# RWKV state update: GpSimd decays the old state and VectorE adds the chunk's products, in place of TensorE's copies of the state into PSUM

## The chip, the cores and the metric

One core of one Trainium2 chip runs the whole program. The time is device microseconds (us) of one execution. Engines are named as in the profile: PE is TensorE (PEld its weight loads), DVE is VectorE, ACT is ScalarE, POOL is GpSimd, SP is SyncE, which here issues DMAs.

## The reference, cut to what matters

The program is a stack of blocks (feed-forward layers, one RWKV mixer, one convolution mixer, two attention and retention blocks). The change lies in the RWKV mixer alone. It has 12 heads of 64 and scans a 64x64 state over 256 context tokens and then 256 latent tokens, once forwards and once backwards:

```python
def wkv_scan(S0, r, w, k, v, kk, bb, reverse):
    ...
    def step(S, inp):
        rt, wt, kt, vt, kkt, bt = inp
        sk = jnp.einsum('bhij,bhj->bhi', S, kkt)
        S = S * wt[:, :, None, :] - sk[..., None] * bt[:, :, None, :] + vt[..., None] * kt[:, :, None, :]
        return S, jnp.einsum('bhij,bhj->bhi', S, rt)

    S, ys = lax.scan(step, S0, xs, reverse=reverse)
    return S, jnp.moveaxis(ys, 0, 1)
...
    for d in range(2):
        ...
        S_c, yc = wkv_scan(S0, r_c, w_c, kd_c, v_c, kk_c, b_c, reverse=(d == 1))
        _, yl = wkv_scan(S_c, r_l, w_l, kd_l, v_l, kk_l, b_l, reverse=(d == 1))
```

## The kernel before, in words

The scan is done in chunks of 64 tokens (`CH`), in float32. Two heads stand together on the 128 partitions (index `x`, 64 partitions each), so there are six pairs of heads, `f` from 0 to 5. For each pair three functions run. `wkv_prepare` makes the pair's projections (the g matmuls on the normed input `y0`, two float16 halves), decays, keys and queries. `wkv_inverse` makes the chunks' 64x64 triangular inverses `SC`: products of keys (KRbd, KBT), 32x32 transposes and a serial loop of small additions on DVE (tiles N and tm), and then small 32x32 matmuls in bank n with ACT copies between them. `wkv_apply` carries the state through eight chunks, `n` from 0 to 7: four of context and four of latents. Both directions `d` go along in each chunk.

One chunk of `wkv_apply`, a step from here on, is a serial chain. PE multiplies the old state (`Sbd` in the trace) by the chunk's keys (tile KR) into bank `b`; ACT copies that into R; PE multiplies R by SC; ACT copies the result into VU; PE multiplies VU by KB into a second bank, `sb`; DVE reads `sb`, multiplies by the chunk's decay `PC`, and writes the new state, from which the next step starts. In the kernel before the old state is in `sb` already: four matmuls by the identity matrix (`ident`) put it there, and the KB products are added to it in PSUM. The state is block diagonal for the two heads, and kept for six chunks (`at` names the buffer of each).

The order on each engine is not written out. A list scheduler places the instructions of all three functions by its own estimates, and each engine then runs its list in order. So while `wkv_apply` of one pair waits in its chain, the projections of the next pair or the out projection, and the key products and transposes of the next inverse, fill PE; they are called fillers below. In the trace all these matmuls have line 232 or 235 (the helpers `mm` and `tr`).

Of the kernel before, what the change touches and what calls it, by code (L numbers as in the profile page):

```python
# [12 lines left out]
OP = mybir.AluOpType  # L13
# [3 lines left out]
P = 128  # L17
# [8 lines left out]
CH = 64  # L26
# [189 lines left out]
class Program:  # L216
# [371 lines left out]
    def run(self):  # L588
        nc, tc, ins = self.nc, self.tc, self.ins
        with ExitStack() as es:  # L590
            self.const = es.enter_context(tc.tile_pool(name="const", bufs=1))
            self.small = es.enter_context(tc.tile_pool(name="small", bufs=1))
            self.psum = es.enter_context(tc.tile_pool(name="ps", bufs=1, space=PSUM))
            self.banks, self.turn, self.bufs = self.BANKS, {}, {"x": 1, "y": 1}
            self.M = [self.const.tile([P, 72, 2], F32, name=f"M{l}") for l in range(2)]
            self.Hl = self.const.tile([P, KD, S], F32, name="Hl")
            self.ones = self.const.tile([P, P], F32, name="ones")
            self.ident = self.const.tile([P, P], F32, name="ident")
            self.eps6 = self.const.tile([P, 1], F32, name="eps6")
            nc.vector.memset(self.ones, 1.0 / D)  # L600
            nc.vector.memset(self.eps6, 1e-6)
            nc.sync.dma_start(self.ident, ins["k_a"][:, 0:P])
            self.sel = self.const.tile([P, 2], F32, name="sel")
            nc.scalar.dma_start(self.sel, ins["k_s"])
            self.craw = self.const.tile([P, KD, 32], F32, name="craw")
            self.cpad = self.const.tile([P, KD, 32], F16, name="cpad")
            self.rst = self.const.tile([P, S], F32, name="rst")
            with ExitStack() as es2:
                E = self.E = {"zi": 0}
                ypool = es2.enter_context(tc.tile_pool(name="y0", bufs=1))  # L610
                opool = es2.enter_context(tc.tile_pool(name="o", bufs=1))
                t = lambda shape, name, dt=F32, pool=ypool: pool.tile(list(shape), dt, name=name)
                self.y0 = t([P, KD, 512], "y0h", F16), t([P, KD, 512], "y0l", F16)
                E["la"], E["reset"] = t([P, 512], "la"), t([P, S], "reset")
                E["zpad"] = [t([P, 2, S + 2], f"zpad{i}") for i in range(2)]
                E["hm"], E["om"] = t([P, 20], "hm"), t([P, 20], "om")
                t([P, 198], "gap")
                E["o"] = t([P, KD, S], "oh", F16, opool), t([P, KD, S], "ol", F16, opool)
                E["sg"] = t([P, S], "sg", F32, opool)
                nc.gpsimd.memset(E["reset"], 1.0)  # L620
                nc.gpsimd.memset(E["reset"][:, ::CH], 0.0)
                for z in E["zpad"]:
                    nc.gpsimd.memset(z, 0.0)
                self.first()
                self.even()
            self.rest()
            self.output()
# [489 lines left out]
    def wkv_apply(self, f):  # L1117

        nc, E = self.nc, self.E
        (SC, SR), (KB, VU), St = E.pop(("chunks", f)), E.pop(("tokens", f)), E["S"]  # L1120
        KR, PC, bon = E["KR", f], E["PC", f], E["bon", f]
        lo = slice(64, 128)
        at = (0, 1, 0, 2, 3, 4, 5)
        uix = lambda q, d, x, c: ((q * 2 + d) * 2 + x) * 4 + c
        for n in range(8):
            q, c = (1, n) if n < 4 else (0, n - 4)
            b = self.bank("w")
            for d in range(2):
                for x in range(2):
                    self.mm(b[lo, d * P + x * CH : d * P + x * CH + CH], SC[0:64, uix(q, d, x, c), 0:64],  # L1130
                            VU[0:64, d, q, c, x * CH : x * CH + CH], d == 0 and x == 0, n == 0)
            for d in range(2):
                if n:
                    self.mm(b[lo, d * P : d * P + P], KR[:, d, q * S + c * CH : q * S + c * CH + CH], St[:, at[n - 1], d, :], False, True)
            if n < 7:
                sb = self.bank("w")
                for x in range(2):
                    h = slice(64 * x, 64 * x + 64)
                    for d in range(2):
                        if n:  # L1140
                            self.mm(sb[h, d * CH : d * CH + CH], self.ident[:, h], St[:, at[n - 1], d, h], d == 0, False)
            R = self.tmp([P, 256], "R")
            nc.scalar.copy(R[lo], b[lo, 0:256])
            for d in range(2):
                for x in range(2):
                    o = d * P + x * CH
                    self.mm(b[lo, 256 + o : 256 + o + CH], SC[lo, uix(q, d, x, c), :], R[lo, o : o + CH], d == 0 and x == 0, True)
            nc.scalar.copy(VU[lo, :, q, c, :], b[lo, 256:512].rearrange("p (d m) -> p d m", d=2))
            if n == 7:
                break  # L1150
            for x in range(2):
                h = slice(64 * x, 64 * x + 64)
                for d in range(2):
                    self.mm(sb[h, d * CH : d * CH + CH], KB[:, d, q, c, h], VU[:, d, q, c, h], n == 0 and d == 0, True)
            for x in range(2):
                h = slice(64 * x, 64 * x + 64)
                nc.vector.tensor_tensor(St[h, at[n], :, h], sb[h, : 2 * CH].rearrange("p (d i) -> p d i", d=2),
                                        PC[h, n, :].unsqueeze(2).to_broadcast([64, 2, CH]), op=OP.mult)
        yb = self.bank("w")
        for cn in range(4):  # L1160
            tt, hh = cn // 2, cn % 2
            rows = slice(64 * hh, 64 * hh + 64)
            o = tt * P
            for d in range(2):
                c = cn if d == 0 else 3 - cn
                self.mm(yb[rows, o : o + P], KR[:, d, 512 + c * CH : 512 + c * CH + CH], St[:, at[3 + c], d, :], d == 0, False)
                for x in range(2):
                    self.mm(yb[rows, o + x * CH : o + x * CH + CH], SR[:, uix(0, d, x, c), :],
                            VU[:, d, 0, c, x * CH : x * CH + CH], False, d == 1)
        y4 = yb[:, :S].rearrange("p (h i) -> p h i", h=4)  # L1170
        mu = self.tmp([P, 4], "mu")
        nc.vector.tensor_reduce(mu, y4, axis=AX.X, op=OP.add)
        nc.vector.tensor_scalar(mu, mu, 1.0 / 64, None, op0=OP.mult)
        yc = self.tmp([P, 4, 64], "yc", bufs=1)
        nc.vector.tensor_tensor(yc, y4, mu.unsqueeze(2).to_broadcast([P, 4, 64]), op=OP.subtract)
        sq = self.tmp([P, 4, 64], "of", bufs=1)
        nc.scalar.activation(sq, yc, AF.Square)
        var = self.tmp([P, 4], "var")
        nc.vector.tensor_reduce(var, sq, axis=AX.X, op=OP.add)
        nc.vector.tensor_scalar(var, var, 1.0 / 64, 64e-5, op0=OP.mult, op1=OP.add)  # L1180
        nc.gpsimd.tensor_tensor(var, var, E["half"].to_broadcast([P, 4]), op=OP.pow)
        nc.vector.tensor_tensor(yc, yc, var.unsqueeze(2).to_broadcast([P, 4, 64]), op=OP.mult)
        tb = self.bank("w")
        for t in range(2):
            self.tr(tb[:, t * P : t * P + P], yc[:, 2 * t : 2 * t + 2, :].rearrange("p h i -> p (h i)"))
        self.mm(tb[:, S:], E["gup", f], E["sg"], False, True)
        of = self.tmp([P, S], "of", bufs=1)
        nc.vector.scalar_tensor_tensor(of, tb[:, :S], self.v("e_gn_w", f, 1), bon, op0=OP.mult, op1=OP.add)
        nc.vector.tensor_tensor(of, of, tb[:, S:], op=OP.mult)
        self.split(E["o"][0][:, f, :], E["o"][1][:, f, :], of)  # L1190
# [716 lines left out]
```

## Time and profile before

| | |
|---|---|
| median of 3 runs | 2735.37 us (2731.1 to 2735.75) |
| the profiled execution's own time | 2735.91 us |
| its span in the profile | 2734.1 us |
| granted TensorE clock, mean | 0.968 |
| PE busy | 2619.9 us, 96% |
| DVE busy | 1749.9 us, 64% |
| ACT busy | 1278.9 us, 47% |
| POOL busy | 423.5 us, 15% |
| the six pairs' steps and inverses | from about 525 to 960 us of the span |

Busy time is the time in which an engine had an instruction in hand. The granted clock is the share of full speed that TensorE was given (1.0 is 2.4 GHz, 0.5 is 1.2 GHz). Matmuls of float32 have two records each in the trace.

### The profile page before, as it was taken

Reading aid. Unit: us, or ns where it says so; the run is one execution under the profiler, and the core shown is the slowest. Engines: PE = TensorE matmul, PEld = TensorE weight load, DVE = VectorE, ACT = ScalarE, POOL = GpSimd, SP = SyncE. Lnnn points to the kernel's source line nnn. Section 1 sums busy time; section 2 is a strip of 40 time slices with the busy share of each in tenths; the row PEclk is TensorE's granted clock in tenths of the full one; section 3 lists DMA queues with packets and bytes.
Section 4 is the critical chain, followed back from the end, with each engine's and each line's share of the span. In section 5 each row is a group of like instructions: output and inputs, shape, how many; then the busy total and the mean of one; then the engine's idle time right before and its main releaser. Section 6 shows DMA issues by size and latency. Waiting matters only on the chain.

```text
span 2734.1 us, 53369 instructions
## 1 busy us (share of the span) xinstructions
PE 2619.9 (96%) x23012; PEld 2009.6 (74%) x23012; DVE 1749.9 (64%) x2601; ACT 1278.9 (47%) x1821; POOL 423.5 (15%) x413
## 2 busy tenths in 40 slices
PE   8999998799999899999989999999999999999998
PEld 4444444476667678888878887888888888888887
DVE  6676676765567366665676556666565666766664
ACT  5454555443344254444645445554544455544443
POOL 0000010321121000199520010000120300000301
PEclk9999999988798899999999999999999999999999
DMA  9676784100102156655626666555656655556563
GB/s 313 240 254 229 263 291 134 53 27 21 32 14 74 40 171 193 208 184 192 182 79 201 193 194 194 169 177 165 214 170 193 200 163 166 171 157 222 170 193 101
DMA packets 427775, 451.71 MB, mean 165 GB/s; under 512 B 9890, under 2 KB 414920, under 8 KB 420243
## 3 DMA queue, kind: packets, MB, share of 16 engines
q1 hardware_dynamic: 422272, 441.29, 50.7%
q10 hardware_dynamic: 5267, 7.01, 0.8%
q8 instruction: 180, 2.95, 0.5%
q14 instruction: 56, 0.46, 0.1%
HBM read 447.18 MB, written 1.08 MB: 164 GB/s over the span
## 4 chain that ended last, share of the span: by engine, by line
PE 60%; DVE 8%; issue 4%; ACT 4%; DMA 2%; POOL 2%; ACTq 0%; SPq 0%; POOLq 0%; DVEq 0%
PE g L232 48%; PE w L232 4%; PE m L232 4%; DVE w L138 3%; PE n L232 2%; ACT w L137 2%; PE m L235 1%; DVE acc L1385 1%; DMA stage<-in_w_in 1%; DVE SC L1057 1%; POOL acc L1391 0%; DMA stage<-in_o_w_in 0%; PE o L232 0%; DVE yl L347 0%; DVE xn L484 0%
## 5 line engine op out<-in xcount | busy, mean ns | idle before, releaser
L232 PEld LDWEIGHTS <-w 128*128 128x128 f16 x14784 | 1440.5, 98 | 447.2 <-issue 96.9
L138 DVE SCALAR_TENSOR_TENSOR w<-stage,w 128x1024 f16<-128x1024 f32 (+2 forms) x812 | 971.6, 1230 | 455.5 <-ACT w L137 453.2
L137 ACT ACTIVATE w<-stage 128x1024 f16<-128x1024 f32 (+2 forms) x812 | 797.7, 1031 | 542.2 <-PE g L232 317.4
L232 PE MATMUL g<-yh,w 128*128 128x256 f16 x5568 | 931.1, 273 | 8.4 <-ACT yh L346 8.3
L232 PE MATMUL g<-yl,w 128*128 128x256 f16 x2784 | 759.1, 273 | 5.6 <-DVE yl L347 5.1
L232 PE MATMUL g<-hh,w 128*128 128x256 f16 (+1 forms) x1936 | 343.0, 282 | 0.0
L232 PE MATMUL g<-hl,w 128*128 128x256 f16 (+1 forms) x968 | 273.4, 282 | 0.0
L232 PE MATMUL g<-y0h,w 128*128 128x512 f16 (+1 forms) x704 | 219.2, 380 | 8.8 <-ACT y0h L346 8.5
L1299 POOL TENSOR_SCALAR diag<-ident,cws 128x128 f16<-128x128 f16 x156 | 144.2, 943 | 8.9 <-DVE cws L1294 8.9
L232 PE MATMUL g<-w,yh 128*128 128x256 f16 (+1 forms) x928 | 138.1, 262 | 0.2 <-ACT ak L1633 0.2
L232 PE MATMUL g<-y0l,w 128*128 128x512 f16 (+1 forms) x352 | 133.8, 381 | 1.3 <-DVE y0l L347 1.3
L232 PE MATMUL g<-w,yl 128*128 128x256 f16 (+1 forms) x464 | 116.5, 262 | 0.0
L311 POOL TENSOR_TENSOR acc<-sq,sq 128x256 f32<-128x256 f32 (+1 forms) x9 | 11.7, 1295 | 625.4 <-ACT sq L753 338.5
L232 PE MATMUL n<-y0h,w 128*128 128x512 f16 x352 | 108.2, 379 | 0.0
L514 ACT ACTIVATE silu<-g 128x512 f32<-128x512 f32 x50 | 29.9, 597 | 155.9 <-issue 135.0
L232 PEld LDWEIGHTS <-yh 128*128 128x128 f16 x928 | 86.9, 98 | 9.4 <-issue 0.9
L232 PE MATMUL g<-ybh,w 128*128 128x256 f16 x512 | 85.2, 273 | 0.0
L516 DVE SCALAR_TENSOR_TENSOR hid<-g,silu 128x512 f32<-128x512 f32 x55 | 38.0, 691 | 68.9 <-PE g L232 64.5
L311 POOL TENSOR_TENSOR acc<-acc,sq 128x256 f32<-128x256 f32 (+1 forms) x45 | 53.9, 1197 | 156.5 <-ACT sq L753 87.4
L1758 POOL TENSOR_TENSOR rst<-rst,epsgn 128x1 f32<-128x1 f32 x16 | 3.0, 189 | 481.4 <-DVE rst L1757 481.4
L232 PE MATMUL g<-ybl,w 128*128 128x256 f16 x256 | 69.8, 273 | 0.0
L311 POOL TENSOR_TENSOR acc<-Hl 128x256 f32<-128x256 f32 x4 | 2.9, 728 | 427.6 <-DVE Hl L1466 427.6
(408 smaller groups left out, 3108.6 us busy)
## 6 DMA issues: line engine op xcount, KB each, us to landing
stage<-in_ffn_w_gu SPq DMA_DIRECT2D x87, 1024.0 KB
stage<-in_ada_w SPq DMA_DIRECT2D x64, 1024.0 KB
stage<-in_w_in SPq DMA_DIRECT2D x64, 1024.0 KB
stage<-in_ffn_w_down SPq DMA_DIRECT2D x32, 1024.0 KB
stage<-in_w_in SPq DMA_DIRECT2D x54, 512.0 KB
stage<-in_w_ffn_gate SPq DMA_DIRECT2D x22, 1024.0 KB
stage<-in_w_ffn_up SPq DMA_DIRECT2D x22, 1024.0 KB
stage<-in_w_ret_proj SPq DMA_DIRECT2D x16, 1024.0 KB
```

The costliest lines, as they stand in the source:

```text
L137: self.nc.scalar.activation(u.t16[:, 0, c], u.stage[:, c], AF.Copy, scale=SW)
L138: self.nc.vector.scalar_tensor_tensor(u.t16[:, 1, c], u.stage[:, c], SW, u.t16[:, 0, c], op0=OP.mult, op1=OP.subtract)
L232: self.nc.tensor.matmul(out, lhsT, rhs, start=start, stop=stop, skip_group_check=True)
L235: self.nc.tensor.matmul(out, in_, self.ident[:k, :k], start=True, stop=True, is_transpose=True, skip_group_check=True)
L311: self.nc.gpsimd.tensor_tensor(acc, state["x"], x, op=OP.add)
L514: nc.scalar.activation(sg, bg, AF.Silu, scale=ISW)
L516: nc.vector.scalar_tensor_tensor(h, bu, ISW, sg, op0=OP.mult, op1=OP.mult)
L1057: nc.vector.transpose(square(h, g), N[quarter(h, g), :, 16 - 16 * g : 48 - 16 * g])
L1299: nc.gpsimd.tensor_scalar(diag[f][:, i, k], id16, w[:, i, k : k + 1], None, op0=OP.mult)
L1385: nc.vector.scalar_tensor_tensor(acc[f], up[:, f, k : k + S], cw[:, f, k : k + 1], acc[f], op0=OP.mult, op1=OP.add)
L1758: nc.gpsimd.tensor_tensor(st[:, 7:8], st[:, 7:8], self.epsgn, op=OP.add)
```

## The change

In chunks 1 to 6 of each pair the four matmuls by the identity go. Two GpSimd instructions per chunk (one for each head) multiply the old state by the chunk's decay into a new tile `kept`, which takes the place of an unused tile of the same size. `sb` then holds the chunk's products alone, and DVE makes the new state as products times decay plus `kept`, in four instructions of 64 columns (head by head, direction by direction), where two of 128 columns stood. Chunk 0 keeps its two DVE instructions.

```diff
@@ run
-                t([P, 198], "gap")
+                E["kept"] = t([P, 198], "kept")[:, :P].rearrange("p (d m) -> p d m", d=2)
@@ wkv_apply
             if n < 7:
                 sb = self.bank("w")
-                for x in range(2):
-                    h = slice(64 * x, 64 * x + 64)
-                    for d in range(2):
-                        if n:
-                            self.mm(sb[h, d * CH : d * CH + CH], self.ident[:, h], St[:, at[n - 1], d, h], d == 0, False)
+                if n:
+
+                    for x in range(2):
+                        h = slice(64 * x, 64 * x + 64)
+                        nc.gpsimd.tensor_tensor(kept[h], St[h, at[n - 1], :, h], PC[h, n, :].unsqueeze(2).to_broadcast([64, 2, CH]), op=OP.mult)
...
-                    self.mm(sb[h, d * CH : d * CH + CH], KB[:, d, q, c, h], VU[:, d, q, c, h], n == 0 and d == 0, True)
+                    self.mm(sb[h, d * CH : d * CH + CH], KB[:, d, q, c, h], VU[:, d, q, c, h], d == 0, True)
...
-                nc.vector.tensor_tensor(St[h, at[n], :, h], sb[h, : 2 * CH].rearrange("p (d i) -> p d i", d=2),
-                                        PC[h, n, :].unsqueeze(2).to_broadcast([64, 2, CH]), op=OP.mult)
+                if n == 0:
+                    nc.vector.tensor_tensor(St[h, at[n], :, h], sb[h, : 2 * CH].rearrange("p (d i) -> p d i", d=2),
+                                            PC[h, n, :].unsqueeze(2).to_broadcast([64, 2, CH]), op=OP.mult)
+                    continue
+                for d in range(2):
+                    nc.vector.scalar_tensor_tensor(St[h, at[n], d, h], sb[h, d * CH : d * CH + CH], PC[h, n, d : d + 1], kept[h, d],
+                                                   op0=OP.mult, op1=OP.add)
```

The scheduler places the program anew. Three places show what it does. The first is PE in the first pair's third chunk, before: `Sbd,KR` are the state's products, `Sbd,ident` the copies, `KRbd,KBT` and `g` fillers, `R,SC`, `VU,KB` and `VU,SC` the rest of the chain.

```order
L232 MATMUL w_4495<-VU_4166,SC_4127 64x64 x4
L232 MATMUL m_4866<-KRbd,KBT_4795 128x256 x2
L232 MATMUL m_4871<-KRbd,KBT_4795 128x256
L232 MATMUL w_4495<-Sbd,KR_4078 64x128 x2
L232 MATMUL w_4502<-Sbd,ident 64x64 x4
L232 MATMUL m_4871<-KRbd,KBT_4795 128x256
L232 LDWEIGHTS w_8_5445
L232 MATMUL g_5470<-y0h,w_8_5445 128x512
L232 MATMUL w_4495<-R_4507,SC_4127 64x64 x4
```

The same place of the changed kernel:

```order
L232 MATMUL w_4495<-Sbd,KR_4078 64x128
L232 MATMUL m_4871<-KRbd,KBT_4795 128x256
L232 MATMUL w_4495<-Sbd,KR_4078 64x128
L232 LDWEIGHTS w_8_5445
L232 MATMUL g_5470<-y0h,w_8_5445 128x512
L232 LDWEIGHTS w_8_5445
L232 MATMUL g_5470<-y0l,w_8_5445 128x512
L232 LDWEIGHTS w_8_5445
L232 MATMUL g_5470<-y0h,w_8_5445 128x512
L232 MATMUL w_4495<-R_4505,SC_4127 64x64 x4
```

The copies are gone, a filler now stands between the two state products, and three g products stand ahead of the R product where one stood.

The second place is PE in the stretch between the fourth pair's steps and the fifth's, where the fifth pair's inverse ends (`T,SC` and `SC,T` are its small matmuls), before:

```order
L232 LDWEIGHTS w_19_7758
L232 MATMUL g_8412<-ol,w_19_7758 128x256
L232 MATMUL n_7377<-T,SC_7125 32x32 x16
L232 MATMUL n_7395<-T,SC_7125 32x32 x16
L232 LDWEIGHTS w_19_7758
L232 MATMUL g_8412<-oh,w_19_7758 128x256
L232 MATMUL n_7413<-SC_7125,T 32x32 x16
L232 MATMUL n_7431<-SC_7125,T 32x32 x16
L232 MATMUL m_7832<-ks_7829,cstA 128x256
L232 MATMUL m_7845<-KRbd,KBT_7791 128x128 x4
```

And in the changed kernel:

```order
L232 MATMUL n_7309<-SC_7125,T 16x16 x64
L232 MATMUL m_7851<-KRbd,KBT_7791 128x128 x4
L232 MATMUL m_7857<-KRbd,KBT_7791 128x256 x2
L232 LDWEIGHTS w_18_7755
L232 MATMUL g_8412<-ol,w_18_7755 128x256
L232 LDWEIGHTS w_18_7755
L232 MATMUL g_8412<-oh,w_18_7755 128x256
L232 MATMUL n_7377<-T,SC_7125 32x32 x16
L232 MATMUL n_7395<-T,SC_7125 32x32 x16
L232 MATMUL m_7862<-KRbd,KBT_7791 128x256
L232 MATMUL n_7413<-SC_7125,T 32x32 x16
L232 MATMUL m_7862<-KRbd,KBT_7791 128x256
```

The long run of g products ahead of `n_7377` (26 in a row before, of which the last stands here) is down to two, and the sixth pair's key products have come in from the fifth pair's steps.

The third place is POOL in the second pair's steps, in the changed kernel (`k`, `v`, `rn` and `kd` belong to the third pair's preparation):

```order
L872 TENSOR_TENSOR k_6209<-zpad_88 128x512
L1142 TENSOR_TENSOR kept<-Sbd,PC_4796 64x128 x10
L872 TENSOR_TENSOR v_6268<-zpad_89 128x512
L944 TENSOR_TENSOR rn_6279<-rn_6279,half 128x8
L1142 TENSOR_TENSOR kept<-Sbd,PC_4796 64x128 x2
L970 TENSOR_TENSOR kd_6304<-kd_6304,k_6209 128x512
```

Before, the same rows stand there without the two of `kept`, in the order k, rn, kd, with v after kd. So the state's 12 GpSimd instructions stand nearly alone in this pair; `rn`, `v` and `kd` wait behind them.

## Rows read from the trace of the kernel before

**Rows 1.** The page: span, and busy time of each engine.

```profile
span 2734.1 us, 53369 instructions
PE 2619.9 (96%) x23012; PEld 2009.6 (74%) x23012; DVE 1749.9 (64%) x2601; ACT 1278.9 (47%) x1821; POOL 423.5 (15%) x413
```

**Rows 2.** Windows: three stretches of steps, then three between; busy us, clock, DMA.

```profile
core 0: us, PE busy (x) PEld busy (x) DVE busy (x) ACT busy (x) POOL busy (x), PEclk, DMA share, GB/s
568.00:608.00 40.00, 39.98 (x382) 26.86 (x383) 27.48 (x72) 15.35 (x31) 4.38 (x4) 1.00 0.06 18
...
788.00:823.00 35.00, 34.94 (x354) 25.63 (x352) 20.80 (x56) 15.70 (x30) 4.35 (x4) 1.00 0.03 9
...
926.50:953.00 26.50, 22.17 (x294) 17.98 (x292) 7.49 (x15) 5.36 (x15) 2.62 (x1) 1.00 0.01 1
```

**Rows 3.** Windows: stretches between the steps of two pairs, same columns.

```profile
608.00:637.00 29.00, 29.00 (x458) 19.53 (x451) 17.38 (x30) 9.89 (x17) 9.09 (x7) 0.57 0.09 24
...
673.00:715.00 42.00, 37.41 (x532) 26.33 (x533) 28.16 (x60) 14.42 (x24) 11.79 (x9) 0.71 0.11 32
...
823.00:863.00 40.00, 36.26 (x550) 26.21 (x548) 30.46 (x64) 17.54 (x29) 11.75 (x9) 0.79 0.34 109
```

**Rows 4.** Timeline: one step of the last pair, with no fillers (start us, us).

```profile
937.94 0.32 PE L232 MATMUL w<-Sbd,KR 128*64 128x128 f32 x1
...
938.69 0.37 ACT L1143 COPY R<-w 64x256 f32<-64x256 f32 x1 [1.96 <-PE w L232]
939.11 0.54 PEld L232 LDWEIGHTS w<-R,SC 64*64 64x64 f32 x8 [0.42 <-ACT R L1143]
...
939.82 0.37 ACT L1148 COPY VU<-w 64x256 f32<-64x256 f32 x1 [0.76 <-PE w L232]
940.24 0.32 PEld L232 LDWEIGHTS w<-VU,KB 128*64 128x64 f32 x8 [0.59 <-ACT VU L1148]
...
940.75 0.59 DVE L1157 TENSOR_TENSOR Sbd<-w,PC 64x128 f32<-64x128 f32 x2 [2.87 <-PE w L232]
941.40 0.13 PEld L232 LDWEIGHTS w<-Sbd,KR 128*64 128x64 f32 x1 [0.23 <-DVE Sbd L1157]
```

**Rows 5.** Timeline: the last pair's last chunk, which has no copies of the state.

```profile
948.31 0.30 PEld L232 LDWEIGHTS w<-Sbd,KR 128*64 128x64 f32 x5 [0.23 <-DVE Sbd L1157]
...
949.05 0.37 ACT L1143 COPY R<-w 64x256 f32<-64x256 f32 x1 [1.96 <-PE w L232]
```

**Rows 6.** Timeline of PE and PEld: a step filled with g products, fourth pair.

```profile
786.86 0.59 PE L232 MATMUL g<-y0h,w 128*128 128x512 f16 x2
787.29 0.38 PE L232 MATMUL g<-y0l,w 128*128 128x512 f16 x1
787.60 0.32 PE L232 MATMUL w<-Sbd,KR 128*64 128x128 f32 x1
...
787.98 0.36 PEld L232 LDWEIGHTS w<-Sbd,ident 128*64 128x64 f32 x4
788.41 0.33 PEld L232 LDWEIGHTS <-w 128*128 128x128 f16 x3
```

**Rows 7.** Timeline of PEld: the same copies at the half clock, third pair.

```profile
722.25 0.66 PEld L232 LDWEIGHTS w<-Sbd,ident 128*64 128x64 f32 x4
```

**Rows 8.** Groups of DVE, 545 to 960 us: busy us, mean ns, idle before.

```profile
L1157 DVE TENSOR_TENSOR Sbd<-w,PC 64x128 f32<-64x128 f32 x84 | 24.2, 288 | 54.1 <-PE w L232 53.2
L138 DVE SCALAR_TENSOR_TENSOR w<-stage,w 128x1024 f16<-128x1024 f32 x17 | 23.5, 1388 | 11.9 <-ACT w L137 11.7
...
L1188 DVE SCALAR_TENSOR_TENSOR of<-w,vec,bon 128x256 f32<-128x256 f32 x6 | 2.9, 483 | 4.8 <-PE w L232 4.7
...
L1175 DVE TENSOR_TENSOR yc<-w,mu 128x256 f32<-128x256 f32 x6 | 2.5, 421 | 0.1
```

**Rows 9.** Groups of POOL, 545 to 960 us, same columns.

```profile
L974 POOL TENSOR_TENSOR KBT<-kd,ep 128x512 f32<-128x512 f32 x9 | 14.5, 1611 | 6.8 <-ACT ep L963 6.5
...
L997 POOL TENSOR_TENSOR ks<-kd,kd 128x256 f32<-128x256 f32 x5 | 3.9, 789 | 0.3
```

More of the change, by code (lines that the diff above doesn't have):

```diff
@@ L1121, in wkv_apply @@
         KR, PC, bon = E["KR", f], E["PC", f], E["bon", f]
+        kept = E["kept"]
         lo = slice(64, 128)
```

## The prediction

> **What bounds the kernel now.** I read the page's head first: the span is 2734.1 us and PE is busy for 96% of it [rows 1]. The change lies in the six pairs' steps, so I read the windows there. In the steps of a pair PE is busy all the time, 39.98 of 40 us and 34.94 of 35, at the full granted clock, while DVE has 20 to 27 us of work and POOL 4 [rows 2]. Only in the last pair's steps, where no fillers are left, PE idles 4.3 of 26.5 us. In the stretches between the steps of two pairs the clock falls to 0.57, 0.71 and 0.79 on average, and PE idles 0, 4.6 and 3.7 us [rows 3]. So the steps are bound by PE's list, not by the chain, except in the last pair; between them it is PE at a lowered clock together with the chain of the inverse (DVE has 30.46 us in 40).
>
> The bare chain stands in the last pair: 3.45 us from one state product to the next (937.94 to 941.40, an idle PE in between) [rows 4]. Of it the DVE update takes 0.59 us, state product to R copy 0.75 us, and R copy to DVE's start 2.06 us.
>
> **What the copies of the state cost.** Chunk 7 has none, and there product to R copy takes 0.74 us [rows 5], with them 0.75 [rows 4]: in the chain they are free. On PE they are not. In a filled step four of the eight loads run after the state products, 0.36 us, and the next filler's load starts behind them (788.41) [rows 6]. At the half clock they take 0.66 us [rows 7]. There are 36 blocks (six chunks, six pairs). In the changed order about seven steps stay without fillers (five of the last pair, two of the fourth), where the freed time is idle time. The other 29 give 29 x 0.36 = 10.4 us, and four that ran at half clock 0.3 us more each: **-11.6 us**.
>
> **The split of the state products.** In 24 steps of the new order a filler stands between the two state products. An entry costs PE: from the last g product to the state product 0.31 us, where a g product takes 0.43 / 2 = 0.215; so 0.095 us, and 0.07 us on the way out (loads end 788.34, next load 788.41) [rows 6]. That is 24 x 0.165 = **+4.0 us**. It is hidden only where PE would wait anyway, and in the steps it hardly does [rows 2]. The Trainium skill, TensorEngine Tiling (Array Packing), Key Properties, says that a change of the tiling mode drains TensorE; state products (128*64) and fillers (128*128) are two modes, so it speaks against this order. The trace agrees, with those 0.095 and 0.07 us; were the drains nothing, the sum would be 4 us better.
>
> **DVE's four instructions for two.** No row has this form. A product of 64 columns from PSUM: 128 columns take 288 ns, 256 take 421 [rows 8], so 1.04 ns a column, and 64 take 221. The nearest row with the same operands (PSUM, a scalar for each partition, an SBUF tile) is L1188, 483 ns for 256 columns, so 283 for 64. Four take 0.88 to 1.13 us, against 0.59. The first state product needs the third of them and the second the fourth, so about 0.22 us of PE's work comes before the end: the bare chain grows by 0.07 to 0.32 us; I take 0.2, as the row with the same operands is the nearer one. In seven bare steps: **+1.4 us** (0.5 to 2.2). In filled steps a filler covers it: the update ends at latest 0.51 + 1.13 = 1.64 us after the start of the KB products, and PE comes to the state product only behind VU,SC and 0.9 to 2.8 us of fillers in the changed order. If that cover were gone, 36 x 0.2 = 7 us. Behind the waiting instruction on DVE stand the next inverse's serial loop and the splits of weights, which PE's fillers wait for; DVE idles 53.2 us in front of this line now [rows 8], and 36 x 0.4 us comes out of that.
>
> **GpSimd.** `kept` needs the old state, ready when the state products start, and DVE needs it 2.81 us later (937.94 to 940.75) [rows 4]. POOL takes 789 ns for 256 columns and 1611 for 512 [rows 9], so 3.2 ns a column and 0.38 us for 128; the upper bound is the 0.79 of 256. A pair takes 0.8 to 1.6 us: 1.2 us or more are to spare. POOL has 4.38 us of work in 40 us of steps [rows 2], and where `kept` stands behind a 1.6 us KBT it is still in time at the lower price. What is queued behind it (rn, v, kd of the next pair) waits for the state at most until the steps end. I cost it at **0**.
>
> **What moved.** Counted in the two orders in products of 512 columns (two of 256 as one), the steps of the six pairs hold 22, 20, 18, 17, 17 and 10 projection products before, and 36, 33, 46, 15, 49 and 3.5 now; the five stretches between hold 27, 46, 35, 50 and 33 before, and 43, 11, 36, 3 and 19.5 now. So 78.5 products go from the stretches into the steps. There they run at the full clock, 78.5 x 0.215 = **+16.9 us**. What the stretches lose is open: at their mean clock of 0.69 a product costs 0.31 us, which would be -24 us; but in two of them 11 and 3 are left, and then DVE's 28 and 30 us [rows 3] bound them. I let the two cancel and take 0.22: **-17.3 us**, bounds 0 and -34 (half clock throughout).
>
> **Sum:** -11.6 + 4.0 + 1.4 + 16.9 - 17.3 = -6.6 us. The profiled execution took 2735.9 us, 0.5 above the median of the runs, so 2729.3; I say **2729**. A measurement of this kernel tells about 0.2%, 5.5 us, from no change.
>
> **The rivals.**
>
> *The moved products pay more than once.* If the stretches shrink by the mean-clock price or the half-clock price, the sum is -13 to -23, 2713 to 2722. For it: all three stretches run at a lowered clock, and one with PE never idle [rows 3]. Against it: DVE's work in the other two.
>
> *The stretches do not shrink (slower).* If the inverse's chain on DVE and ACT already sets their length, the 16.9 us in the steps are simply added: between -6.6 + 17.3 = +10.7 and half of that, 2741 to 2747. It decides from where the stretches give back less than 10.7 us. For it: 30.46 us of DVE in 40, and key products of the next inverse that now stand in the stretch; against it: PE idle there is only 9 to 11% [rows 3].
>
> *GpSimd and DVE hold each other up.* DVE's wide splits (1388 ns [rows 8]) read two SBUF tiles as `kept` does. A pair of `kept` that waits for one of them ends 0.8 + 1.4 = 2.2 to 3.0 us after the state, at the edge of 2.81; and each `kept` can hold a DVE instruction for 0.4 to 0.8 us. In half of the steps, 18 x 0.5 = +9 us: 2738. Against it: 1611 ns for 512 columns is about twice the 789 of 256, so no such surplus shows on average [rows 9]. The Trainium skill, SBUF — State Buffer, SBUF: two separate sides, has VectorE instructions with two SBUF inputs and GpSimd instructions that read SBUF shut each other out for a whole instruction; no row here shows that apart.
>
> *Nothing comes of it.* The freed time turns into waits of PE for the inverse: 2735.
>
> **How the numbers follow.** Forecast 0.42 (its own range 2723 to 2735), moved products pay more 0.22, stretches do not shrink 0.17, hold-up 0.10, nothing 0.09. Faster by over 0.2% (under 2729.9): 0.22 and just over half of the forecast's, 0.45. Slower by over 0.2%: 0.17 and half of the hold-up, 0.22. The rest, 0.33, is within. The range takes in both outer cases but their ends: 2714 to 2744.
>
> **What would show it.** The groups must have no `Sbd,ident`, four DVE instructions of 64 columns a chunk at 0.22 to 0.29 us, and 72 of `kept` at 0.38 to 0.79. The last pair's bare step should be 3.5 to 3.8 us, its DVE update released by PE and not by POOL. In the windows, the steps of the first three pairs and of the fifth should grow by some 1 to 6 us each, and the second and fourth stretch between pairs should shrink. I am wrong if these stretches keep their length, if many updates are released by POOL, or if PE's clock falls within the steps.

## The result and the profile after

The changed kernel took 2750.1 us (median; 2744.9 to 2753.4), the kernel before 2733.3 beside it: ratio 1.0065, 95% interval 1.0048 to 1.0083. It is slower, where 2729 was forecast. The page of after, against [rows 1]:

```profile
span 2742.8 us, 53048 instructions
...
PE 2616.2 (95%) x22724; PEld 2000.4 (73%) x22724; DVE 1760.9 (64%) x2673; ACT 1279.2 (47%) x1821; POOL 450.8 (16%) x485
```

PE has 3.7 us less work and 288 instructions fewer, and the span is 8.7 us longer. So I looked at where PE waits, and at which clock it works. The windows of after follow the work: from a pair's second R copy to its eighth (six steps, odd rows), and on to the next pair's second R copy (the stretch between, even rows). Columns are those of [rows 2].

```profile
568.65:604.62 35.97, 35.17 (x281) 21.39 (x282) 25.14 (x75) 15.58 (x31) 10.41 (x16) 1.00 0.07 19
604.62:642.89 38.27, 33.64 (x539) 22.86 (x537) 24.52 (x48) 15.12 (x24) 8.30 (x9) 0.82 0.12 31
642.89:678.95 36.06, 35.28 (x300) 22.95 (x301) 24.26 (x72) 15.45 (x29) 9.88 (x14) 1.00 0.12 34
678.95:717.56 38.61, 29.76 (x523) 24.21 (x522) 27.33 (x58) 12.92 (x22) 7.42 (x9) 0.73 0.11 31
717.56:752.92 35.36, 34.49 (x281) 20.59 (x281) 26.96 (x75) 17.48 (x32) 13.06 (x18) 1.00 0.06 16
752.92:790.97 38.05, 34.73 (x546) 24.33 (x545) 24.75 (x48) 12.64 (x22) 5.52 (x7) 0.87 0.09 25
790.97:824.16 33.19, 30.36 (x257) 20.26 (x258) 24.20 (x71) 14.79 (x30) 9.78 (x14) 0.93 0.03 9
824.16:865.54 41.38, 35.35 (x521) 28.68 (x520) 25.48 (x51) 10.56 (x19) 6.57 (x7) 0.62 0.01 2
865.54:896.33 30.79, 30.70 (x293) 21.37 (x293) 19.99 (x62) 13.24 (x25) 5.57 (x10) 0.97 0.25 76
896.33:929.08 32.75, 30.70 (x533) 23.09 (x532) 12.98 (x21) 8.56 (x16) 2.97 (x2) 0.69 0.13 44
929.08:956.49 27.41, 21.80 (x182) 17.11 (x182) 6.20 (x25) 4.41 (x13) 6.33 (x13) 0.62 0.00 1
```

The same windows of a kernel that has the old order and the time of before (a_gpsimd_alone, below). I measure against it, since the trace of before itself had more half clock than the other traces of that order (116 us from the first pair's second R copy to the last pair's, against 89 here).

```profile
571.69:603.26 31.57, 31.55 (x287) 20.36 (x284) 23.48 (x63) 13.90 (x28) 6.18 (x13) 1.00 0.06 18
603.26:637.96 34.70, 34.70 (x533) 24.10 (x532) 19.79 (x36) 11.08 (x19) 11.16 (x10) 0.70 0.10 27
637.96:668.21 30.25, 30.23 (x298) 22.10 (x296) 18.36 (x48) 11.71 (x23) 5.33 (x12) 1.00 0.04 15
668.21:712.54 44.33, 38.99 (x586) 28.02 (x584) 29.94 (x69) 17.69 (x29) 13.57 (x12) 0.81 0.10 30
712.54:742.03 29.49, 29.46 (x294) 21.51 (x291) 18.98 (x49) 13.70 (x26) 6.30 (x12) 1.00 0.13 38
742.03:779.95 37.92, 34.39 (x549) 23.46 (x547) 28.20 (x54) 14.85 (x26) 11.80 (x10) 0.82 0.06 18
779.95:809.24 29.29, 29.29 (x295) 21.60 (x292) 17.85 (x44) 11.86 (x24) 7.49 (x13) 1.00 0.03 10
809.24:854.24 45.00, 41.20 (x602) 29.59 (x601) 33.45 (x76) 21.02 (x35) 13.95 (x12) 0.81 0.10 31
854.24:881.85 27.61, 27.54 (x298) 21.27 (x295) 18.40 (x52) 10.65 (x23) 4.00 (x10) 1.00 0.11 32
881.85:918.38 36.53, 33.27 (x564) 25.80 (x562) 15.53 (x27) 10.13 (x18) 3.09 (x2) 0.72 0.21 66
918.38:940.81 22.43, 18.25 (x239) 14.29 (x236) 7.33 (x14) 4.41 (x13) 8.05 (x13) 1.00 0.10 33
```

Add the rows. The steps of pairs 1 to 5 go from 148.2 to 171.4 us (+23.2): PE's busy time by 17.9, its waits from 0.1 to 5.4. The five stretches go from 198.5 to 189.1 (-9.4): PE's busy time falls by 18.4, but its waits grow from 15.9 to 24.9. The last pair goes from 22.4 to 27.4 (+5.0), and there the clock falls from 1.00 to 0.62. Together +18.8 us in these windows. The two spans differ by 11.9 us only (after is 3.0 us shorter ahead of the windows and 3.8 behind them), the medians by 16.8: each trace is one execution.

The last pair's bare step in the timeline of after, against [rows 4]:

```profile
941.88 0.37 ACT L1144 COPY R<-w 64x256 f32<-64x256 f32 x1 [2.93 <-PE w L232]
942.30 0.92 PEld L232 LDWEIGHTS w<-R,SC 64*64 64x64 f32 x8 [0.91 <-ACT R L1144]
...
944.70 0.99 DVE L1163 SCALAR_TENSOR_TENSOR Sbd<-w,PC,kept 64x64 f32<-64x64 f32 x4 [3.87 <-PE w L232]
945.31 0.93 POOL L1142 TENSOR_TENSOR kept<-Sbd,PC 64x128 f32<-64x128 f32 x2 [3.94 <-DVE Sbd L1163]
...
946.75 0.37 ACT L1144 COPY R<-w 64x256 f32<-64x256 f32 x1 [2.93 <-PE w L232]
```

DVE's update waits for PE, not for POOL, and takes 0.99 us, as forecast. But a step takes 4.87 us (941.88 to 946.75) where 3.45 stood: the eight R loads take 0.92 us in place of 0.54, and the granted clock is 0.50 from 935.54 to 962.84 us, so PE is at 1.2 GHz.

PE's waits in after, in the pairs (us in total, times, longest):

```profile
PE w L235 <- DVE yc L1188: 14.4, 4, 7.5
PE w L232 <- ACT VU L1149: 3.7, 8, 0.5
PE m L232 <- ACT KRbd L1021: 3.6, 1, 3.6
PE w L232 <- ACT R L1144: 3.6, 7, 0.5
PE n L232 <- DVE T L1060: 3.4, 4, 2.2
```

And in a_gpsimd_alone:

```profile
PE n L232 <- DVE T L1060: 11.5, 7, 2.7
```

The old order waits mostly for the inverse (T), and briefly. The new one stands at the transposes of yc (the end of a pair's output), which it has ahead of the next inverse's small matmuls. Splitting the second and the fourth stretch of after where the large group of these matmuls begins (693.54 and 839.94 us) shows what bounds either part:

```profile
678.95:693.54 14.59, 6.51 (x66) 4.64 (x64) 12.88 (x28) 5.49 (x9) 5.35 (x5) 0.75 0.00 0
693.54:717.56 24.02, 23.24 (x457) 19.56 (x458) 14.44 (x31) 7.43 (x13) 2.06 (x4) 0.72 0.18 49
824.16:839.94 15.78, 9.75 (x66) 7.77 (x65) 13.54 (x24) 3.22 (x6) 5.11 (x4) 0.61 0.01 2
839.94:865.54 25.60, 25.60 (x455) 20.92 (x456) 11.94 (x28) 7.34 (x13) 1.46 (x3) 0.63 0.01 3
```

In the first part DVE is busy for 12.88 of 14.59 us and 13.54 of 15.78, and PE waits for it. In the second PE is hardly ever idle. Key products (28 and 26 records, where a_gpsimd_alone has 0 and 12) stand there in place of most of the g products, and much of it runs at 1.2 GHz.

### The profile page after: what moved, and what is told of

It is laid out like the page before. It is cut to its first block, busy times and chain, and to the rows that moved or that the text cites. A ratio compares the mean times of both kernels' runs of the same rounds, so it can differ in the third digit from the quotient of the medians.

```text
span 2742.8 us, 53048 instructions
## 1 busy us (share of the span) xinstructions
PE 2616.2 (95%) x22724; PEld 2000.4 (73%) x22724; DVE 1760.9 (64%) x2673; ACT 1279.2 (47%) x1821; POOL 450.8 (16%) x485
## 4 chain that ended last, share of the span: by engine, by line
PE 79%; DVE 10%; ACT 4%; issue 3%; POOL 2%; DMA 2%; ACTq 0%; SPq 0%; POOLq 0%; DVEq 0%
PE g L232 56%; PE n L232 8%; PE w L232 7%; PE m L232 5%; DVE w L138 3%; ACT w L137 2%; PE m L235 1%; DVE acc L1391 1%; DVE SC L1057 1%; DVE xn L484 1%; POOL acc L1397 0%; DMA stage<-in_o_w_in 0%; PE o L232 0%; DMA stage<-in_ffn_w_gu 0%; POOL rn L944 0%
## 5 line engine op out<-in xcount | busy, mean ns | idle before, releaser
L311 POOL TENSOR_TENSOR acc<-sq,sq 128x256 f32<-128x256 f32 (+1 forms) x9 | 11.9, 1324 | 625.2 <-ACT sq L753 338.4
```

The costliest lines, as they stand in the source:

```text
L311: self.nc.gpsimd.tensor_tensor(acc, state["x"], x, op=OP.add)
```

## The experiments

All 15 in one table, then one by one. Times in us from one trace each: steps of pairs 1 to 5, the five stretches, the last pair's six steps (windows as above). Ratios are against the kernel before on the same chip, with 95% interval.

| kernel | PE order | ratio | steps | stretches | last pair |
|---|---|---|---|---|---|
| before, first trace | old | 1 | 155.3 | 202.7 | 22.3 |
| a_gpsimd_alone | old | 1.0003 [0.9988, 1.0017] | 148.2 | 198.5 | 22.4 |
| b_copies_out_old_order | old | 1.0015 [0.9998, 1.0032] | 149.1 | 196.8 | 27.5 |
| d_four_dve_old_order | old | 1.0024 [1.0006, 1.0042] | 148.2 | 192.8 | 26.7 |
| b_after_old_order | old | 1.0023 [1.0009, 1.0036] | 149.1 | 201.2 | 28.5 |
| c_last_pair_as_before | old | 0.9990 [0.9973, 1.0007] | 144.7 | 199.1 | 22.3 |
| after, first trace | new | 1.0065 [1.0048, 1.0083] | 171.4 | 189.1 | 27.4 |
| c_after_again | new | 1.0079 [1.0051, 1.0106] | 177.3 | 197.3 | 27.4 |
| c_after_unsplit | new | 1.0054 [1.0033, 1.0074] | 169.6 | 192.9 | 27.4 |
| d_after_yc_later | new | 1.0112 [1.0084, 1.0141] | 177.5 | 198.6 | 27.4 |
| d_after_yc_unsplit | new | 1.0141 [1.0109, 1.0172] | 178.1 | 203.1 | 29.1 |
| a_dve_alone | new, own | 1.0091 [1.0076, 1.0106] | 180.5 | 188.7 | 27.2 |
| a_dummy_copies | as a_dve_alone | 1.0082 [1.0065, 1.0100] | 181.6 | 182.9 | 25.1 |
| b_before_new_order | as a_dve_alone | 1.0081 [1.0059, 1.0103] | 180.7 | 182.7 | 26.8 |
| a_copies_out | new, own | 1.0033 [1.0014, 1.0051] | 159.3 | 197.4 | 30.4 |
| b_after_dead_products | as after | 1.0112 [1.0091, 1.0133] | 175.8 | 196.9 | 35.7 |
| c_after_dead_f16 | as after | 1.0096 [1.0065, 1.0126] | 177.2 | 197.8 | 35.7 |

Theories: *order* (the scheduler's new places cost it), *clock* (TensorE loses its clock in the last pair), *hold-up* (GpSimd and DVE block each other).

**One part alone**, placed by the scheduler. a_gpsimd_alone:

```diff
+                        nc.gpsimd.tensor_tensor(kept[h], St[h, at[n - 1], :, h], PC[h, n, :]..., op=OP.mult)
```

> The kernel before, with the 72 GpSimd products into kept that nothing reads. PE's order is that of before word for word. Theory order: within 3 us of before. Theory clock: the same. Theory hold-up: 8 to 15 us slower, DVE's additions of the inverse and its splits longer in the mean.

No difference: GpSimd's part costs nothing, and hold-up falls. a_dve_alone:

```diff
+                nc.gpsimd.memset(E["kept"], 0.0)
...
-                nc.vector.tensor_tensor(St[h, at[n], :, h], sb[h, : 2 * CH]..., op=OP.mult)
+                for d in range(2):
+                    nc.vector.scalar_tensor_tensor(St[h, at[n], d, h], sb[h, d * CH : d * CH + CH], PC[h, n, d : d + 1], kept[h, d], ...)
```

> The kernel before with the four DVE instructions of 64 columns (their added tile holds zeros, nothing writes it again); PE's copies stay, GpSimd has nothing new. PE's order has 27 split state products and 59.5 products of 512 columns more in the steps than before. Theory order (the four DVE instructions make the scheduler place PE anew, and that order is the loss): 10 to 25 us slower than before. Theory clock (PE without its copies falls to half clock in the last pair's bare steps): bare step 3.6 to 3.8 us at full clock, total within 6 us of before. Theory hold-up (GpSimd and DVE shut each other out): within 6 us of before.

As slow as the whole change, or slower (1.0091; the two measurements of after have 1.0065 and 1.0079, and the intervals overlap). a_copies_out:

```diff
-                            self.mm(sb[h, d * CH : d * CH + CH], self.ident[:, h], St[:, at[n - 1], d, h], d == 0, False)
```

> The kernel before without the copies of the state: the old state's own term is left out of the update, so only the time counts. DVE keeps its two instructions, and no state product is split in PE's order. Theory order: 5 to 15 us faster than before, since PE's freed time counts in filled steps. Theory clock: the last pair's bare steps at half clock, 4.3 to 4.9 us each, and the total 3 to 10 us slower than before or the same.

Slower although PE has less to do: all six steps of the last pair are at half clock. a_dummy_copies is the changed kernel with the four copies put back as dead work:

> The changed kernel with PE's copies put back as dead work: they are written into sb ahead of the chunk's products, which overwrite them. PE's order is that of a_dve_alone word for word. Theory order: as slow as a_dve_alone within 4 us, so 10 to 25 us over before. Theory clock: the bare steps come back to 3.6 to 3.8 us at full clock, and the total is within 6 us of before. Theory hold-up: 8 to 15 us over a_dve_alone.

As slow as a_dve_alone. It keeps the full clock for three bare steps (3.78, 3.73, 3.72 us) and then falls to 4.87.

**Order and arithmetic apart.** From here on most kernels have their order written out: a table of places (for the old order 432 runs of instructions on PE) taken from another kernel's program, chained after all instructions are traced. Line numbers are therefore higher.

```diff
         Program(tc, aps, out).run()
+        for engine, runs in ORDERS.items():
+            queue = [i for i in nc.cur_bb.bb.instructions if str(i.engine) == "EngineType." + engine ...]
+            at, last = 0, None
+            for skip, count in runs:
+                at += skip
+                for i in queue[at : at + count]:
+                    if last is not None:
+                        tc.add_manual_dep(i, last.name, mybir.DependencyInfo(mybir.DependencyClass.NoSync, ...), reason="order")
+                    last = i
+                at += count
```

> The kernel before (copies on PE, two instructions of VectorE, no kept), with its instructions placed by hand in the order of a_dve_alone on PE, DVE, ACT and POOL. The arithmetic is that of before to the last instruction. Theory order: it is slow like a_dve_alone, 2750 to 2757, with steps near 36, 40, 37, 35, 30 us. Rival (the four instructions of VectorE cost it, by their own length): it is back at 2733, and the steps at 31 to 32 us. In between, the two share the 24 us: what is above 2733 is the order's part, and what is left up to 2757.9 is that of the instructions. Clock: with two instructions of VectorE the last pair's bare steps should be 3.45 us again if the share of PE in the chain keeps the clock.

2756.3 against 2734.4: the arithmetic of before, to the last instruction, loses 22 us by its order alone (the order is that of a_dve_alone, not that of after). Its steps grow by 32 us over the old order, its stretches shrink by 16.

> The changed kernel's instructions (no copies, GpSimd's kept, four instructions of VectorE) with the order of the kernel before written out by hand on PE, DVE, ACT and POOL; kept stands where it stood in a_gpsimd_alone, which had the order of before. Theory order (the loss is where the scheduler placed PE's work anew): the loss is gone. The old order without the copies should take 2733 less up to the 11.6 us of the freed copies, 2721 to 2733; if TensorE falls to half clock in the last pair's steps here too, some 6 us of that are lost again, 2727 to 2735. Rival (the four instructions of VectorE themselves, or the lost copies, cost it): it stays at 2745 to 2755, and the steps of pairs 1, 2 and 4 stay at 33 us and more. Rows to look at: steps of the six pairs (31.6, 31.5, 35.4, 29.3, 27.6, 22.3 us before), bare steps of the last pair (3.45 before, 4.87 after).

2741.7: the order is worth 0.4 to 0.6% (1.0065 and 1.0079 against 1.0023), 11 to 15 us. The kernel still takes 7 us more than before, where it was expected to gain or to break even: the last pair takes 28.5 us for 22.4.

> As a_copies_out (the old state's term is left out: no copies, two instructions of VectorE, no kept), but with the order of the kernel before by hand on PE, DVE, ACT and POOL. The only difference from the kernel before is that 144 copies are not there. Theory order: it gains up to what was forecast for the copies, 11.6 us, 2721 to 2727, less what a lower clock takes. Rival (without the copies TensorE loses its clock in the bare steps, whatever the order): the last pair's steps stay at 4.87 us, which takes 6 us or more of the gain, 2727 to 2735. If the copies cost nothing on PE in the filled steps, 2733 to 2740.

2740.7, no gain either. Bare steps: 3.47 at full clock, then 4.43 and 4.87.

> As a_dve_alone (copies on PE, four instructions of VectorE with a kept that is zero, so that the sum adds nothing), but in the order of the kernel before by hand on PE, DVE, ACT and POOL. It is the fourth of four kernels in the old order: copies or none, two instructions of VectorE or four. The instructions themselves should cost 0.25 us a step only where nothing fills it, five steps of the last pair. Theory clock A (the lost copies take the clock in the last pair): it keeps the clock, bare steps of 3.7 us, 2733 to 2737. Theory clock B (the longer VectorE takes it as well): bare steps at 4.87 us after one to three at full clock, 2739 to 2744.

At full clock the filled steps are those of before to 0.01 us (5.29, 5.39, 4.85, 4.55, 5.37, 6.14 in the first pair): there the longer update costs nothing. Bare steps take 3.65 and 3.64, so +0.19; then the clock falls, with the copies present (4.66, 4.87, 4.87). Theory B held for the clock: in the old order, copies out or a longer update, either takes it (one trace each). The median, 2734.9, lies in A's range, but before took 2727.7 beside it.

> Pairs 1 to 5 in the changed form (no copies, kept on GpSimd, four instructions of VectorE), the last pair as before (copies on PE, two instructions of VectorE), all in the order of the kernel before, by hand on PE, DVE, ACT and POOL. In b_after_old_order the five filled pairs' steps took 6.3 us less than before and the last pair's 6.2 us more, at half clock. Theory (the last pair's chain without copies is what loses the clock): its bare steps are at 3.45 us again, the 6.3 us stay, and the kernel takes 2725 to 2731, faster than before and than the changed one. Rival (the clock that is missing there is only pushed on, or the gain is lost in the stretches between): 2733 to 2740.

```diff
-                if n == 0:
+                if n == 0 or f == 5:
                     nc.vector.tensor_tensor(St[h, at[n], :, h], ...)
```

(and the copies under `if n and f == 5`). The last pair's window is at full clock again; the same window of b_after_old_order stands behind it:

```profile
913.00:935.31 22.31, 18.24 (x239) 14.29 (x236) 7.33 (x14) 4.41 (x12) 2.37 (x1) 1.00 0.01 2
```

```profile
919.61:948.13 28.52, 23.00 (x195) 17.75 (x194) 9.64 (x26) 4.41 (x12) 8.05 (x13) 0.66 0.00 1
```

9 us between the two ratios (0.33% of 2734), 6.2 of them in these windows. It is the best kernel of the study, but the gain that was expected cannot be told from nothing: 0.9990, interval 0.9973 to 1.0007.

**Holding the clock with dead work**, behind the KB products of the last pair:

```diff
+            if f == 5 and n:
+                for d in range(2):
+                    self.mm(sb[:, 256:512], self.ident, St[:, at[n - 1]].rearrange("p d m -> p (d m)"), True, True)
```

> The changed kernel in its own order, held by hand on four engines, with two dead products (identity by state, 256 columns, into unused columns of the bank) behind the KB products of chunks 1 to 6 of the last pair only: 12 more products, whose result nobody reads. They stand where PE waits for VectorE. Theory clock: TensorE stays at full clock there, the five bare steps take 3.7 to 3.9 us in place of 4.87, and the kernel takes 5 to 6 us less than the changed one, 2743 to 2746. Rival (4.87 us is the longer chain of VectorE and GpSimd and not the clock): the bare steps stay at 4.87 us or grow, 2750 or more.

```diff
+                for d in range(4):
+                    self.mm(sb[:, 256:512], E["o"][0][:, 0, :P], E["o"][0][:, 1, :], True, True)
```

> As b_after_dead_products (the changed kernel in its own order, by hand on four engines), but the dead work behind the KB products of the last pair's chunks 1 to 6 is four float16 products of 256 columns each, as the projections' are, in place of two float32 products of 256 columns: a fraction of the time on PE, 24 products in all. [...] Theory fillers (it is the float16 products that keep TensorE at full clock in the filled steps): the bare steps take 3.7 to 3.9 us in place of 4.87, and the kernel some 5 us less than the changed one, 2743 to 2747. Rival (no dead work helps, the clock follows the length of the chain): 4.87 us and 2750 again.

Neither comes near 3.9 us a step, but neither tests the clock. The dead products write unused columns of the bank that DVE's update reads, and the update waits for them: both traces have the row `DVE Sbd L1243: 30.7, 6` under who waited for the dead products (us, times). They stand in the chain, not beside it. The float32 ones have a stretch at full clock in the middle, where after has none:

```profile
950.92:957.75 6.83, 4.54 (x45) 3.18 (x45) 0.96 (x4) 1.47 (x4) 0.85 (x3) 1.00 0.00 0
```

A step there takes 4.77 us (951.33 to 956.10), so the 3.7 to 3.9 could not have come out at either clock. With the float16 ones the clock had fallen at 922.30, 25 us before the first dead product (947.13), and it stays down for the whole window:

```profile
943.80:979.50 35.70, 30.86 (x206) 22.17 (x207) 6.20 (x25) 4.41 (x12) 6.17 (x13) 0.50 0.00 1
```

Whether work beside the chain would hold the clock stays open.

**Inside the new order.** Splits closed, 24 times:

```diff
 w<-Sbd,KR 64x128
-g<-y0h,w 128x512
 w<-Sbd,KR 64x128
+g<-y0h,w 128x512
```

> The changed kernel in its own order, by hand on PE, DVE, ACT and POOL, with one edit: in the 24 steps in which a filler stands between the two state products it stands behind the second one. The prediction put 0.165 us on each split, the trace after shows about 0.25 us. Theory split: 4 to 6 us less than the changed kernel, 2744 to 2746. Rival (a filler in between costs nothing, since the second product waits for the fourth instruction of VectorE anyway): no difference, 2750, or slightly more where PE now waits for that instruction.

> The changed kernel once more, as the measure for the other three on the same chip, and for a second trace: 2750 (2745 to 2753 in its first four runs), ratio near 1.0065. Its first profiled run, 2744.9 us, was the fastest of four, so the trace showed 9 of the 17 us; this one should show whether the rest lies in the stretches at half clock between the pairs (137.0 us of half clock in the pairs then) and behind the last pair, or in the steps (each within 0.3 us of the first trace if not).

The fifth pair's steps at full clock fall from 4.85 and 4.86 us to between 4.56 and 4.61, 0.25 to 0.29 for a split. In the whole kernel 1.0054 against 1.0079, intervals that overlap: the 4 to 6 us are not shown. The second trace of after has 2770.3 us, its longest run: 136.5 us of half clock in pairs 1 to 5 and their stretches where the first had 102.4 (with the last pair 123.3, not 137.0), the same waits otherwise.

> The changed kernel with PE in its own order by hand, but for one edit: after pairs 1 and 2 the two yc transposes (with the gup product, and the first four VU,SC products of the next pair, which stand just behind) stand behind small matmuls of the next inverse in place of ahead of them: behind its second group for pair 1, in the middle of its third for pair 2. The other engines are scheduled by the program's own scheduler and differ in some 30 places around it. In the trace after PE waits 4.5 and 7.5 us at these two places, 12 of the 14.4 us that it waits for yc. Theory waits (what makes the new order slow is PE's new waits, 14 us more idle time in the first five pairs, most of it here): 8 to 12 us less than the changed kernel, 2739 to 2744. Rival (the wait only moves: the inverse's chain on DVE and ACT sets the end of the stretch): 2748 to 2754, with the idle time at PE's small matmuls in place of yc.

```diff
-w<-ident,yc x2, w<-sg,gup, n<-T,SC, w<-VU,SC x4, n<-T,SC x63 ...
+n<-T,SC x64, ..., w<-ident,yc x2, w<-sg,gup, w<-VU,SC x4
```

The rival held, and the time (2765.0) lies even above its range. The 12 us of waits for yc are gone, and PE stands at the inverse instead:

```profile
PE n L268 <- DVE T L1096: 19.5, 7, 9.5
...
PE w L271 <- DVE yc L1224: 2.8, 2, 2.0
```

3.4 became 19.5 us, and the time did not fall (1.0112). DVE ends the inverse's transposes T 14.9 and 15.6 us into the first and the second stretch, as in after. So the yc transposes only stood first in a queue that had nothing else to do.

> As d_after_yc_later, and the 24 splits of the state products closed as in c_after_unsplit, PE by hand, the other engines scheduled. If waits and splits add up, another 2 to 5 us less, 2735 to 2741: all that then is left against the kernel before is the last pair's clock (some 9 us by b_after_old_order against c_last_pair_as_before), less the freed copies. Rival (the new order loses by the work that it moves and not by waits and splits): 2748 or more.

No faster (the intervals overlap), with two new waits (11.4 us for KRbd, ACT's copy of the keys, and 5.5 for DVE's split of a weight into float16 halves); the other engines were placed anew around it. It says nothing on the splits.

## Why the prediction was wrong

**What moved** is the step that failed: "I let the two cancel and take 0.22". What the stretches would lose was argued from a price of a product. PE's work did leave them, 18.4 us of busy time where I wrote 17.3. Their length fell by 9.4 only, since PE's waits in them grew by 9.0: the first part of a stretch is as long as the inverse's chain on DVE and ACT, and where the fillers are gone PE waits for it (DVE busy for 12.88 of 14.59 us and 13.54 of 15.78; d_after_yc_later). The second and fourth stretch, which lost 35 and 47 products by my count, are 5.7 and 3.6 us shorter. This was my second rival, in the place it named; its 2741 to 2747 fell short of the 2750 measured. Half clock also rose in the stretches, from 88.7 to 96.0 us, most of all in the fourth (17.1 to 31.1); how much of their length is the clock and not the chain was not tested apart. Nor had I counted all that moves. Of PE's records in the steps of pairs 1 to 5, key products (KRbd,KBT) fall from 130 to 33; transposes rise from 120 to 180, the la,lora products from 8 to 32 (0.64 us each), projection products from 110 to 255. And the steps, where I had PE hardly ever wait, got 5.2 us more of waits: 0.5 to 0.8 us for GpSimd's rn in each of the first four pairs, and the chain itself in the fourth, whose last steps are bare now.

**The copies**: -11.6 us was too much. In the same order, with four DVE instructions and copies or without (d_four_dve_old_order, c_last_pair_as_before), pairs 1, 3, 4 and 5 take 0.9, 0.8, 1.4 and 1.0 us less without: 4.1 us in 24 steps, 0.17 each and not 0.36. The most that a step gains is 0.23 us, in 14 of them: 0.36 us was the time of the loads, and PE was not held for all of it. Five gain 0.02 us, and there PE now idles for 0.14 to 0.19 us: the chain sets the time.

**The split** was right in kind and small: 0.25 to 0.29 us for 0.165. The Trainium skill, TensorEngine Tiling (Array Packing), Key Properties, has the drain at a change of mode; closing the splits agrees with it, by that quarter of a microsecond.

**Four DVE instructions**: +0.19 us in a bare step for 0.2, nothing in a filled one, both as forecast. Missed was what hangs on it: "wrong if PE's clock falls within the steps". It fell: a bare step takes 4.87 us where the same instructions take 3.73 at full clock (b_after_old_order), and the last pair +5.0 us for +1.4 forecast in all.

**GpSimd at 0** was right: `kept` takes 439 ns on average (0.38 to 0.79 forecast), and hardly ever ends an update's wait:

```profile
L1142 POOL TENSOR_TENSOR kept<-Sbd,PC 64x128 f32<-64x128 f32 x72 | 31.6, 439 | 159.5 <-DVE Sbd L1163 96.1 <-DVE Sbd L1159 59.5 <-POOL kept L1142 0.3
```

```profile
L1163 DVE SCALAR_TENSOR_TENSOR Sbd<-w,PC,kept 64x64 f32<-64x64 f32 x144 | 34.6, 280 | 53.7 <-PE w L232 52.4
```

By size: steps +23.2 for the +9.3 of copies, splits and moved work; stretches -9.4 for -17.3; last pair +5.0 for +1.4. The three differences make 25.4 us, and -6.6 becomes +18.8. In the steps, 7.5 of the 13.9 us are the copies (4.1 for 11.6, as measured in the old order), 5.2 the waits and some 2.5 the splits (24 x 0.27 for 4.0). So no one term carries the miss: the copies are as large as the stretches. Some of the steps' growth is the clock in the fourth pair (0.93 in its window); that was not tested apart. Nor are the sizes more than those of one execution: in the second trace of after the stretches take 197.3 us, 1.2 less than the old order's 198.5, and the steps 177.3.

## What to carry to other kernels

Where a list scheduler places the program, a change is two changes: its arithmetic and a new order. Hold the order by hand and measure them apart: here the order cost 11 to 15 us and the arithmetic without the last pair nothing that could be told. Filler work is worth most in the stretch that waits for another engine: before it is credited for leaving one, ask what that stretch waits for next. And work on PE beside a chain that costs the chain nothing may still be what its clock rests on: look at the granted clock of the barest stretch first. A test with dead work must keep it out of the chain, or it measures the chain.

## What the runs showed of the hardware

Two traces with the same order on all engines (before, and a_gpsimd_alone, which adds only `kept`) differ by 11 us: 358.0 and 346.7 us from the first pair's second R copy to the last pair's. Of that 116.1 and 88.7 us are at half clock; filled steps that are at full clock in both agree to 0.01 us. In the old order the bare steps keep 3.46 us to the end in three traces (before, a_gpsimd_alone, c_last_pair_as_before), and fall to 4.87 after one or two of them in the three in which 0.2 us are added on DVE, 0.36 us of loads are taken off PE, or both (d_four_dve_old_order, b_copies_out_old_order, b_after_old_order). The arithmetic of before fell too in an order with 7 projection products in the last pair's steps where 20 stood (b_before_new_order: 3.55, 3.79, 4.87). The Trainium skill, TensorE: Matmul & The Clock Gate, Part 1, lets the clock follow how busy PE has been; these falls agree with that (PE is busy for 2.62 of 3.45 us in a bare step of before, and for 2.62 of 3.64 in the step of d_four_dve_old_order ahead of its fall). The window of c_after_dead_f16 (0.50 throughout, at 30.86 of 35.70 us busy) does not bear it out, though half clock itself lengthens the records that make up that busy time.

DVE and GpSimd do shut each other out, only too seldom to matter. In b_after_old_order a weight split that takes 1.23 us elsewhere takes 3.44 us beside a wide GpSimd instruction. The timelines of DVE and of POOL:

```profile
919.62 3.44 DVE L138 SCALAR_TENSOR_TENSOR w<-stage,w 128x1024 f16<-128x1024 f32 x1 [1.11 <-ACT w L137]
```

```profile
918.38 3.60 POOL L515 TENSOR_TENSOR KB<-KB,gs 128x2048 f32<-128x2048 f32 x1 [24.17 <-PE n L303]
```

In after 5 of the 72 `kept` take 0.69 to 1.47 us in place of 0.39, each beside a DVE instruction that reads two SBUF tiles, three of them beside weight splits. The Trainium skill, SBUF — State Buffer, SBUF: two separate sides, has this lock for a whole instruction; these rows agree.
